# A feed-forward block on one Trainium2 core: a third set of raw weight buffers, Silu left in its PSUM bank, and a multiplication moved from GpSimd to VectorE

## The chip, the cores and the metric

The kernel runs on one core of a Trainium2 chip. The core has five engines that each follow their own list of instructions in order: TensorE (PE; its weight loads are listed apart as PEld), VectorE (DVE), ScalarE (ACT), GpSimd (POOL) and SyncE (SP), whose list here is almost only DMA issues. They wait for each other through semaphores. The time is device microseconds (us) of one execution; the number given for a kernel is the median of several runs.

## The reference

A trunk of two layers over 512 positions of width 1024, all in float32. Layer 0 has a sparse attention mixer, layer 1 a sliding-window mixer; behind each mixer stands the same feed-forward block, which is what the change touches:

```python
def causal_depthwise_conv(a, w, bias):
    ...  # over time, width 3, one filter per channel
    return y + bias.astype(a.dtype)

def conv_ffn(h, w_gu, conv_w, conv_b, w_down):
    a, u = jnp.split(h @ w_gu, 2, axis=-1)
    a = causal_depthwise_conv(a, conv_w, conv_b)
    return (jax.nn.silu(a) * u) @ w_down

for i in range(DEPTH):
    h = rms_norm(x, norm_mix[i])
    ...  # x = x + nsa_mixer(h, ...) in layer 0, x = x + swa_mixer(h, ...) in layer 1
    h = rms_norm(x, norm_ffn[i])
    x = x + conv_ffn(h, ffn_w_gu[i], ffn_conv_w[i], ffn_conv_b[i], ffn_w_down[i])
return rms_norm(x, norm_final)
```

`w_gu` is 1024 x 5632 (2816 columns for a, 2816 for u), `w_down` is 2816 x 1024.

## The kernel before

Activations lie transposed: features on the 128 partitions, the 512 positions along a row. Every float32 product is made from three products of rounded parts: an operand is split into a high part (rounded, written by ACT) and a low part (the difference to the original, written by DVE or POOL), and high x high, high x low and low x high are summed in PSUM.

The feed-forward block, function `ffn`, works on 22 tiles f of 128 channels of a and u. The first three (`PLAIN`) are done by `gate_up`, with whole 1024-row products (line L205). The other 19 are done by `gate_up_7`: the four half products of a tile (two halves of the positions by two halves of the input rows, for a and u) come from seven products over 256 positions (L619, 12 matmuls each, 84 for a unit) instead of eight, in the manner of Strassen and Winograd. One such tile is called a unit below. For a unit:

- `weights(f)` loads four raw quarter tiles a1, a2, u1, u2 of 128 x 512 (256 KB each, DMAs issued by SP, L591). POOL makes four sums and differences of them (L596): s1 = u1+u2, s2 = s1-a1, s3 = a1-u1, s4 = a2-s2. s2 and s3 share one buffer, named `wraw` in the rows.
- Each of the seven weights a1, s2, s3, a2, s1, s4, u2 is split: ACT writes the high part (L602: ha, wh, hs, hu), DVE the low part (L608: la, wl, ls, lu). For a1, a2 and u2 ACT first copies the raw weight to PSUM (L607), so that DVE reads one input from PSUM and one from SBUF; for s1, s2, s3, s4 (the rows ls and wl) DVE reads both inputs from SBUF. u2 is the last of the seven in program order.
- PE makes the seven products into the banks mm, s, t and o; ACT and DVE sum them into `apad` and into u's tile (L623, L629, L637; in the rows u's tile is called g, xh or xl).
- `activate` forms the convolution in a PSUM tile of the name t: one ACT instruction (L536) and two of DVE (L537, L538); then ACT applies Silu (L539) into an SBUF tile y, of which there is one buffer. At L649 (L555 in the plain units) POOL multiplies u by y.

All raw quarters have two buffers each (`BUFS`: a1, a2, u1, u2, and s1 and s4 too); `wraw` also has two. A DMA into a buffer waits until the last reader of the tile that lay there is done. Once the units are done, the low halves of the 22 gated tiles are put into the buffers that the weights have left, in the order of the list `GL`, and `down` multiplies by w_down.

The order of instructions on each engine isn't written out by hand: the framework's scheduler sets it when the kernel is built, from dependences, buffers and its own estimate of times. On the chip each engine keeps to its list, so an instruction that waits holds everything behind it on that engine.

Of the kernel before, what the change touches and what calls it, by code (L numbers as in the profile page):

```python
# [11 lines left out]
F32 = mybir.dt.float32  # L12
F32R = mybir.dt.float32r
AF = mybir.ActivationFunctionType
ALU = mybir.AluOpType
AX = mybir.AxisListType

P = 128
T = 512
# [38 lines left out]
PLAIN = (3, 3)  # L58
OPER = ((0, 1, 1, 1), (0, 1, 1, 1))
PLO = ((3, 6, 7), (3, 6))  # L60
BUFS = dict(a1=2, a2=2, u1=2, u2=2, s1=2, s4=2, ha1=2, la1=2, ha2=1, la2=1, hs1=1, ls1=1, hs4=1, ls4=1, hu2=1, lu2=1)
GL = [n for n in ("u1", "a1", "u2", "a2", "s1", "s4", "ha1", "la1", "ha2", "la2", "hs1", "ls1", "hs4", "ls4") for _ in range(BUFS[n])]
BANKS = dict(a1=("mm", B_MM), a2=("s", B_S), u2=("t", B_T))
CUES = (((), (0, 1), (2, 3, -1), (4, 5), (6, 7), (), ()), ((), (0, 1, 2), (3,), (4, 5, 6, -1), (7, 8), (), ()))
# [441 lines left out]
def ffn(tc, layer, e):  # L506
    nc, wp, ps, V = e["nc"], e["wp"], e["ps"], e["V"]
# [4 lines left out]
    with tc.tile_pool(name=f"ffn{layer}", bufs=1) as pool:  # L512
# [3 lines left out]
        def conv(i):  # L516
            return conv_t[:, i:i + 1]
# [4 lines left out]
        def gated(f):  # L522
            k = f - NF + len(x_tags)
            n = f"g{f}" if k < 0 else f"{x_tags[k][0]}{x_tags[k][1]}"
            g[f] = (pool if k < 0 else e["cp"]).tile([P, T], F32, name=n, tag=n)
            return g[f]
# [4 lines left out]
            nc.vector.memset(t[:, 0:2], 0.0)  # L531

        def activate(f, a):
            y = pool.tile([P, T], F32, name="y", tag="y", bufs=1)
            py = ps.tile([P, T], F32, name="t", tag="t", bufs=B_T)
            nc.scalar.activation(py, a[:, 2:], AF.Identity, scale=conv(f * 3 + 2), bias=conv(3 * NF + f))  # L536
            nc.vector.scalar_tensor_tensor(py, a[:, 1:T + 1], conv(f * 3 + 1), py, op0=ALU.mult, op1=ALU.add)  # L537
            nc.vector.scalar_tensor_tensor(py, a[:, 0:T], conv(f * 3), py, op0=ALU.mult, op1=ALU.add)  # L538
            nc.scalar.activation(y, py, AF.Silu)  # L539
            return y  # L540

        def plain(f, j, tag):
            w = load_w(e["w_gu"][layer, j, f], DM, nc.gpsimd if 2 * f + j in PLO[layer] else None)
            with tc.issue_after(e["stats"].behind.ins) if f == 1 and j == 0 else nullcontext():
                return run_value(e["proj_steps"](w=w, tag=tag))

        def gate_up(f):
            pa = plain(f, 0, "mm") if f else e["first"][0]
            a = apad[f % 2]
            nc.vector.tensor_tensor(a[:, 2:], pa, rstd, op=ALU.mult)  # L550
            y = activate(f, a)
            pu = plain(f, 1, "s") if f else e["first"][1]
            u = gated(f)
            nc.vector.tensor_tensor(u, pu, rstd, op=ALU.mult)
            nc.gpsimd.tensor_tensor(u, u, y, op=ALU.mult)  # L555

# [2 lines left out]
        def half(n, dt=F32R):  # L561
            return pool.tile([P, T], dt, name=n, tag=n, bufs=BUFS[n])

# [23 lines left out]
        def weights(f):  # L587
            a1, a2, u1, u2, s1, s4 = (half(n, F32) for n in ("a1", "a2", "u1", "u2", "s1", "s4"))
            for j, h, w in ((0, 0, a1), (1, 0, u1), (1, 1, u2), (0, 1, a2)):
                with tc.high_priority(offset=100):  # L590
                    nc.sync.dma_start(w, e["w_gu"][layer, j, f, :, h * T:(h + 1) * T])  # L591
            s23, l23, h23 = (wp.tile([P, 2, T], t, name=n, tag=n) for n, t in (("wraw", F32), ("wl", F32R), ("wh", F32R)))
            s2, s3 = (s23[:, h] for h in range(2))
            for out, x, y, op in ((s1, u1, u2, ALU.add), (s2, s1, a1, ALU.subtract), (s3, a1, u1, ALU.subtract),
                                  (s4, a2, s2, ALU.subtract)):
                nc.gpsimd.tensor_tensor(out, x, y, op=op)  # L596
            ws = {1: (h23[:, 0], l23[:, 0]), 3: (h23[:, 1], l23[:, 1])}
            for o, n, w in ((0, "a1", a1), (1, None, s2), (3, None, s3), (5, "a2", a2), (2, "s1", s1), (6, "s4", s4),
                            (4, "u2", u2)):
                if n:  # L600
                    ws[o] = half("h" + n), half("l" + n)
                nc.scalar.copy(ws[o][0], w)  # L602
                if n in BANKS:

                    tag, bufs = BANKS[n]
                    w = ps.tile([P, T], F32, name=tag, tag=tag, bufs=bufs)
                    nc.scalar.copy(w, {"a1": a1, "a2": a2, "u2": u2}[n])  # L607
                nc.vector.tensor_tensor(ws[o][1], w, f32(ws[o][0]), op=ALU.subtract)  # L608
            return ws

        def gate_up_7(f, cue):
            ws = weights(f)
            pa, pb, pc, pd = (ps.tile([P, T], F32, name=n, tag=n, bufs=b)[:, :H]
                              for n, b in (("mm", B_MM), ("s", B_S), ("t", B_T), ("o", B_O)))

            def product(pt, o, start=False):
                ops = [(0, x, i) for i in range(NK // 2) for x in range(2)] + [(1, 0, i) for i in range(NK // 2)]
                for n, (w, x, i) in enumerate(ops):
                    nc.tensor.matmul(pt, ws[o][w][:, i * P:(i + 1) * P], xs[:, o, i, x], start=start and n == 0,  # L619
                                     stop=n == len(ops) - 1, skip_group_check=True)  # L620

            def add(dst, pt, src):
                nc.vector.tensor_tensor(dst, pt, src, op=ALU.add)  # L623

            a, u = apad[f % 2], gated(f)
            al, ar = a[:, 2:2 + H], a[:, 2 + H:]
            ul, ur = (u[:, c] for c in HALVES)
            product(pa, 0, True)
            nc.scalar.copy(ar, pa)  # L629
            cue(0)  # L630
            product(pb, 1, True)
            add(ul, pb, ar)
            cue(1)
            product(pc, 3, True)
            cue(2)
            product(pa, 5)
            nc.scalar.copy(al, pa)  # L637
            cue(3)
            product(pb, 2)
            add(ar, pb, ar)  # L640
            add(ur, pc, ar)
            cue(4)
            product(pd, 6, True)
            add(ar, pd, ar)
            cue(5)
            product(pc, 4)
            add(ul, pc, ul)
            cue(6)
            nc.gpsimd.tensor_tensor(u, u, activate(f, a), op=ALU.mult)  # L649

        prs = ps.tile([P, T], F32, name="t", tag="t", bufs=B_T)
        nc.scalar.copy(prs, rstd)
        for f in range(PLAIN[layer]):
            gate_up(f)
            for i in range(NK // 2):
                if OPER[layer][i] == f:
                    operands(i)
        for f in range(PLAIN[layer], NF - 1):
            gate_up_7(f, lambda n: None)
# [20 lines left out]
        def cue(n):  # L680
            for f in CUES[layer][n]:
                if f < 0:
                    w_down.append(load_down(0, -1 - f))
                else:
                    split_g(f)

        gate_up_7(NF - 1, cue)

        stats = Stats(e["pool"], nc.gpsimd, 3) if layer == 0 else Stats(pool, nc.gpsimd, 3)
# [875 lines left out]
```

## Time and profile before

| what | value |
|---|---|
| median of 3 runs | 1295.8 us (1295.52 to 1297.48) |
| profiled execution | 1297.73 us |
| its span, first to last instruction | 1295.9 us |
| granted TensorE clock, mean | 0.982 |
| PE busy | 1228.0 us (95%) |
| DVE busy | 939.0 us (72%) |
| ACT busy | 760.1 us (59%) |
| POOL busy | 604.7 us (47%) |

The shares are means over very different stages. The two feed-forward blocks begin at about 372 and 910 us of the span; in each the plain units and the preparation of operands come first, then 19 units of seven products, then the down projection. Each row of the trace names an engine, a line of the kernel, and output and input tiles (out<-in).

### The profile page before, as it was taken

How to read it: one execution, taken by the hardware profiler on the slowest of the kernel's cores; microseconds unless marked ns; L12 is line 12 of the kernel's file. 1: busy time of each engine (PE TensorE's matmuls, PEld its weight loads, DVE VectorE, ACT ScalarE, POOL GpSimd, SP SyncE). 2: the span in 40 equal slices, each digit the busy share in tenths (PEclk: the TensorE clock that was granted, in tenths of full speed). 3: DMA queues.
4: the chain of work that ended last, by engine and by line, in shares of the span. 5: the costliest groups of instructions: out<-in, count | busy, mean ns of one | idle time of the engine just before them, and what ended most of it. 6: DMA issues, size and time to landing. Idle time of an engine off the chain costs nothing.

```text
span 1295.9 us, 20370 instructions
## 1 busy us (share of the span) xinstructions
PE 1228.0 (95%) x7246; PEld 1058.7 (82%) x7246; DVE 939.0 (72%) x1799; ACT 760.1 (59%) x1584; POOL 604.7 (47%) x451
## 2 busy tenths in 40 slices
PE   7999999989998999999999998999989999999997
PEld 5867986877876999999888886778779999998886
DVE  6376777978688897999633367897888999994223
ACT  4276667767558666767422225866677676683222
POOL 4494554523239676664100137322577766730002
PEclk9999999989998999999999998999989999999999
DMA  5856635041232332332233345322423332223333
GB/s 196 227 159 191 199 103 153 26 142 37 62 104 99 95 103 92 104 92 62 80 99 90 108 156 157 106 82 90 132 75 97 98 106 92 81 69 90 95 101 122
DMA packets 66485, 141.70 MB, mean 109 GB/s; under 512 B 8528, under 2 KB 16976, under 8 KB 66384
## 3 DMA queue, kind: packets, MB, share of 16 engines
q1 hardware_dynamic: 65008, 139.25, 35.5%
q8 instruction: 57, 0.93, 0.3%
q10 hardware_dynamic: 1376, 1.15, 0.3%
q14 instruction: 44, 0.36, 0.1%
HBM read 123.14 MB, written 17.24 MB: 108 GB/s over the span
## 4 chain that ended last, share of the span: by engine, by line
PE 53%; DVE 19%; DMA 7%; POOL 7%; ACT 7%; issue 5%; SPq 1%; POOLq 0%; DVEq 0%; ACTq 0%
PE mm L205 29%; PE t L619 4%; PE s L619 3%; DVE wl L608 3%; PE mm L619 3%; DMA u<-in_w_gu 2%; PE s L1165 2%; POOL s L596 2%; DVE ls L608 2%; PE o L619 2%; PE o L1007 2%; PE t L1189 2%; POOL wraw L596 1%; DMA d<-rh 1%; PE o L1307 1%
## 5 line engine op out<-in xcount | busy, mean ns | idle before, releaser
L182 ACT CAST wh<-wraw 128x1024 fp32r<-128x1024 f32 (+3 forms) x132 | 122.2, 926 | 224.5 <-PE mm L205 139.2
L183 DVE TENSOR_TENSOR wl<-wraw,wh 128x1024 fp32r<-128x1024 f32 (+3 forms) x80 | 98.0, 1225 | 118.7 <-PE mm L205 72.2
L183 POOL TENSOR_TENSOR wl<-wraw,wh 128x1024 fp32r<-128x1024 f32 (+3 forms) x52 | 98.7, 1902 | 136.5 <-PE mm L205 67.2
L205 PE MATMUL mm<-xs,wh 128*128 128x512 f32 (+1 forms) x374 | 141.5, 382 | 0.0
L238 POOL TENSOR_TENSOR rt<-rt 128x512 f32<-128x512 f32 x22 | 31.5, 1430 | 192.2 <-ACT rt L232 192.0
L608 DVE TENSOR_TENSOR wl<-wraw,wh 128x512 fp32r<-128x512 f32 x76 | 97.2, 1282 | 18.8 <-ACT wh L602 18.6
L205 PE MATMUL mm<-xh,wh 128*128 128x512 f32 x248 | 102.1, 413 | 6.9 <-ACT wh L182 5.1
L205 PE MATMUL mm<-xl,wh 128*128 128x512 f32 x248 | 99.9, 404 | 2.1 <-DVE xl L306 2.0
L619 PE MATMUL mm<-xs,ha 128*128 128x256 f32 x608 | 92.5, 289 | 9.4 <-ACT apad L629 4.8
L619 PEld LDWEIGHTS mm<-xs,ha 128*128 128x128 f32 x608 | 81.8, 195 | 12.3 <-ACT apad L629 6.2
L205 PE MATMUL mm<-xs,wl 128*128 128x512 f32 (+1 forms) x374 | 90.6, 382 | 0.0
L602 ACT CAST wh<-wraw 128x512 fp32r<-128x512 f32 x76 | 46.8, 620 | 69.4 <-POOL wraw L596 57.2
L1175 ACT ACTIVATE p<-p,sm 128x128 f32<-128x128 f32 (+3 forms) x128 | 71.7, 562 | 20.1 <-DVE sm L1172 19.5
L205 PEld LDWEIGHTS mm<-xs,wh 128*128 128x128 f32 x374 | 70.3, 188 | 14.7
L608 DVE TENSOR_TENSOR ls<-s,hs 128x512 fp32r<-128x512 f32 x76 | 80.2, 1060 | 0.0
L205 PEld LDWEIGHTS mm<-xs,wl 128*128 128x128 f32 x374 | 67.7, 188 | 15.1
L1172 DVE CUSTOM_DVE_ANT_0 p<-s,cst 128x128 f32<-128x128 f32 (+3 forms) x128 | 58.3, 480 | 18.1 <-PE t L1189 10.4
L205 PE MATMUL mm<-xh,wl 128*128 128x512 f32 x248 | 67.7, 403 | 0.0
L596 POOL TENSOR_TENSOR s<-u,u 128x512 f32<-128x512 f32 x38 | 53.2, 1401 | 27.1 <-DMA u<-in_w_gu 21.5
L649 POOL TENSOR_TENSOR xl<-xl,y 128x512 f32<-128x512 f32 x16 | 29.6, 1852 | 77.4 <-ACT y L539 69.9
L205 PEld LDWEIGHTS mm<-xh,wh 128*128 128x128 f32 x248 | 48.5, 196 | 18.8 <-ACT wh L182 5.3
L596 POOL TENSOR_TENSOR s<-a,wraw 128x512 f32<-128x512 f32 x38 | 62.8, 1653 | 0.2
(369 smaller groups left out, 3689.1 us busy)
## 6 DMA issues: line engine op xcount, KB each, us to landing
u<-in_w_gu SPq DMA_DIRECT2D x76, 256.0 KB, 2.9
a<-in_w_gu SPq DMA_DIRECT2D x76, 256.0 KB, 2.8
wraw<-in_w_dn SPq DMA_DIRECT2D x34, 512.0 KB, 3.5
wraw<-in_w_nsa SPq DMA_DIRECT2D x19, 512.0 KB, 4.9
q<-d SPq DMA_DIRECT2D x32, 256.0 KB, 5.1
wraw<-in_w_dn SPq DMA_DIRECT2D x17, 384.0 KB, 3.1
wraw<-in_w_gu SPq DMA_DIRECT2D x12, 512.0 KB, 3.5
d<-rh SPq DMA_DIRECT2D x21, 256.0 KB, 2.2
```

The source lines that it names most:

```text
L182: nc.scalar.copy(wh[:, c], raw[:, c])
L183: (eng or lo_eng[0]).tensor_tensor(wl[:, c], raw[:, c], f32(wh[:, c]), op=ALU.subtract)
L205: nc.tensor.matmul(pt, ws[k][w], rs[k][r], start=first and i == 0, stop=last and i == len(ops) - 1, **kw)
L238: self.eng.tensor_tensor(self.acc, self.acc, sq, op=ALU.add)
L596: nc.gpsimd.tensor_tensor(out, x, y, op=op)
L602: nc.scalar.copy(ws[o][0], w)
L608: nc.vector.tensor_tensor(ws[o][1], w, f32(ws[o][0]), op=ALU.subtract)
L619: nc.tensor.matmul(pt, ws[o][w][:, i * P:(i + 1) * P], xs[:, o, i, x], start=start and n == 0, stop=n == len(ops) - 1, skip_group_check=True)
L649: nc.gpsimd.tensor_tensor(u, u, activate(f, a), op=ALU.mult)
L1007: nc.tensor.matmul(acc[0][:, j * P:], v2[:, 2 * j + br], pp[:, 4 * j:4 * j + NT - j, :], start=br == 0 and j == 0 and pp is pts[0][0], sto ...
L1172: nc.vector.tensor_tensor_reduce(pt[:, c], pss[:, c], mask[:, T - (c.stop - c.start):], -1.0, 3e38, ALU.add, ALU.min, st[:, u:u + 1])
L1175: nc.scalar.activation(pt[:, c], pt[:, c], AF.Exp, scale=-1.0, bias=st[:, u:u + 1], accum_out=st[:, 2 + u:3 + u])
```

## The change

The four raw quarters get a third buffer each. Silu writes back into the PSUM tile that it reads, and the SBUF tile y is gone. The multiplication of u by it is issued by VectorE instead of GpSimd, in the plain units and in the units of seven products. A scratch area for dynamic DMAs is made smaller when the program is built, which leaves room in SBUF. `GL` is made from `BUFS`, so its first twelve places are now the raw quarters, and hs1, ls1, hs4 and ls4 are no longer used for low halves.

```diff
-BUFS = dict(a1=2, a2=2, u1=2, u2=2, s1=2, s4=2, ha1=2, la1=2, ha2=1, la2=1, hs1=1, ls1=1, hs4=1, ls4=1, hu2=1, lu2=1)
+BUFS = dict(a1=3, a2=3, u1=3, u2=3, s1=2, s4=2, ha1=2, la1=2, ha2=1, la2=1, hs1=1, ls1=1, hs4=1, ls4=1, hu2=1, lu2=1)
...
         def activate(f, a):
-            y = pool.tile([P, T], F32, name="y", tag="y", bufs=1)
             py = ps.tile([P, T], F32, name="t", tag="t", bufs=B_T)
...
-            nc.scalar.activation(y, py, AF.Silu)
-            return y
+            nc.scalar.activation(py, py, AF.Silu)
+            return py
...
             nc.vector.tensor_tensor(u, pu, rstd, op=ALU.mult)
-            nc.gpsimd.tensor_tensor(u, u, y, op=ALU.mult)
+            nc.vector.tensor_tensor(u, u, y, op=ALU.mult)
...
-            nc.gpsimd.tensor_tensor(u, u, activate(f, a), op=ALU.mult)
+            nc.vector.tensor_tensor(u, u, activate(f, a), op=ALU.mult)
...
-    nc = bacc.Bacc("TRN2", target_bir_lowering=False, num_devices=1)
+    nc = bacc.Bacc("TRN2", target_bir_lowering=False, num_devices=1, dynamic_dma_scratch_size=4096)
```

Lines behind L539 have a number one smaller in the changed kernel (L648 for L649, L607 for L608). The lists of the two mixers stay as they were; inside the feed-forward blocks the scheduler orders anew. POOL's list before, two units in the middle of layer 0 (the numbers behind the names tell the tiles of one unit from those of the next):

```order
L596 TENSOR_TENSOR s4_5452<-a2_5448,wraw_5457 128x512
L649 TENSOR_TENSOR xh3_5198<-xh3_5198,y_5290 128x512
L596 TENSOR_TENSOR s1_5601<-u1_5599,u2_5600 128x512
L596 TENSOR_TENSOR wraw_5607<-s1_5601,a1_5597 128x512
L596 TENSOR_TENSOR wraw_5757<-a1_5747,u1_5749 128x512
L596 TENSOR_TENSOR s4_5602<-a2_5598,wraw_5607 128x512
L649 TENSOR_TENSOR xh4_5348<-xh4_5348,y_5440 128x512
L596 TENSOR_TENSOR s1_5751<-u1_5749,u2_5750 128x512
```

And POOL's list now, over about the same units:

```order
L595 TENSOR_TENSOR s1_5589<-u1_5587,u2_5588 128x512
L595 TENSOR_TENSOR wraw_5595<-s1_5589,a1_5585 128x512
L595 TENSOR_TENSOR wraw_5744<-a1_5734,u1_5736 128x512
L595 TENSOR_TENSOR s4_5590<-a2_5586,wraw_5595 128x512
L595 TENSOR_TENSOR s1_5738<-u1_5736,u2_5737 128x512
L595 TENSOR_TENSOR wraw_5744<-s1_5738,a1_5734 128x512
L595 TENSOR_TENSOR s4_5739<-a2_5735,wraw_5744 128x512
L595 TENSOR_TENSOR wraw_5893<-a1_5883,u1_5885 128x512
L595 TENSOR_TENSOR s1_5887<-u1_5885,u2_5886 128x512
```

The multiplication no longer stands between one unit's four sums and the next one's. DVE's list before, from one unit's low parts to the next one's:

```order
L608 TENSOR_TENSOR wl_5758<-wraw_5757,wh_5759 128x512
L623 TENSOR_TENSOR xh6_5648<-s_5645,apad0_3990 128x256
L537 SCALAR_TENSOR_TENSOR t_5591<-apad1_3991,conv_t_3988,t_5591 128x512
L538 SCALAR_TENSOR_TENSOR t_5591<-apad1_3991,conv_t_3988,t_5591 128x512
L623 TENSOR_TENSOR xh5_5498<-t_5496,xh5_5498 128x256
L608 TENSOR_TENSOR lu2_5639<-t_5641,hu2_5638 128x512
L608 TENSOR_TENSOR la2_5775<-s_5777,ha2_5774 128x512
L608 TENSOR_TENSOR la1_5915<-mm_5917,ha1_5914 128x512
L623 TENSOR_TENSOR apad0_3990<-s_5645,apad0_3990 128x256
L608 TENSOR_TENSOR ls1_5781<-s1_5751,hs1_5780 128x512
L623 TENSOR_TENSOR xh6_5648<-t_5646,apad0_3990 128x256
L608 TENSOR_TENSOR wl_5908<-wraw_5907,wh_5909 128x512
```

And DVE's list now, first up to the last sum into a unit's u, then from its multiplication on to the low parts of a later unit:

```order
L607 TENSOR_TENSOR ls4_5623<-s4_5590,hs4_5622 128x512
L607 TENSOR_TENSOR la2_5613<-s_5615,ha2_5612 128x512
L607 TENSOR_TENSOR wl_5745<-wraw_5744,wh_5746 128x512 x2
L622 TENSOR_TENSOR apad1_3991<-s_5484,apad1_3991 128x256
L607 TENSOR_TENSOR ls1_5619<-s1_5589,hs1_5618 128x512
L607 TENSOR_TENSOR la1_5752<-mm_5754,ha1_5751 128x512
L622 TENSOR_TENSOR xh5_5487<-t_5485,apad1_3991 128x256
L622 TENSOR_TENSOR apad1_3991<-o_5486,apad1_3991 128x256
L622 TENSOR_TENSOR xh6_5636<-s_5633,apad0_3990 128x256
L536 SCALAR_TENSOR_TENSOR t_5579<-apad1_3991,conv_t_3988,t_5579 128x512
L537 SCALAR_TENSOR_TENSOR t_5579<-apad1_3991,conv_t_3988,t_5579 128x512
L622 TENSOR_TENSOR xh5_5487<-t_5485,xh5_5487 128x256
```

```order
L648 TENSOR_TENSOR xh5_5487<-xh5_5487,t_5579 128x512
L607 TENSOR_TENSOR lu2_5627<-t_5629,hu2_5626 128x512
L607 TENSOR_TENSOR la2_5762<-s_5764,ha2_5761 128x512
L622 TENSOR_TENSOR apad0_3990<-s_5633,apad0_3990 128x256
L607 TENSOR_TENSOR ls1_5768<-s1_5738,hs1_5767 128x512
L607 TENSOR_TENSOR la1_5901<-mm_5903,ha1_5900 128x512
L622 TENSOR_TENSOR xh6_5636<-t_5634,apad0_3990 128x256
L607 TENSOR_TENSOR wl_5894<-wraw_5893,wh_5895 128x512
L622 TENSOR_TENSOR apad0_3990<-o_5635,apad0_3990 128x256
L607 TENSOR_TENSOR wl_5894<-wraw_5893,wh_5895 128x512
L607 TENSOR_TENSOR ls4_5772<-s4_5739,hs4_5771 128x512
```

The multiplication (L648) now stands in DVE's list behind the last sum into u; the low parts around it have changed places among each other and with the sums.

## Rows read from the trace of the kernel before

**Rows 1.** Busy time by stretch: us, PE, PEld, DVE, ACT, POOL, clock, DMA share, GB/s.

```profile
372.00:420.00 48.00, 40.97 (x200) 33.69 (x200) 39.88 (x58) 35.92 (x65) 34.98 (x31) 0.92 0.34 111
420.00:470.00 50.00, 50.00 (x409) 49.92 (x409) 42.22 (x70) 34.60 (x67) 34.39 (x24) 0.97 0.33 100
470.00:619.00 149.00, 140.83 (x1137) 137.49 (x1137) 134.18 (x199) 102.15 (x195) 95.26 (x62) 1.00 0.28 87
619.00:741.00 122.00, 122.00 (x530) 98.19 (x529) 49.37 (x54) 37.88 (x49) 13.54 (x9) 1.00 0.31 92
...
1012.00:1161.00 149.00, 141.93 (x1144) 138.06 (x1145) 138.20 (x198) 103.28 (x196) 96.60 (x63) 1.00 0.29 88
```

**Rows 2.** Waits, 470 to 619 us: who for whom, us in total, times, longest.

```profile
ACT wh L602 <- POOL wraw L596: 22.0, 11, 3.9
...
PE t L619 <- DVE xh L623: 3.1, 3, 1.4
```

**Rows 3.** POOL by form, 470 to 619 us: busy, mean ns | idle before, releaser.

```profile
L596 POOL TENSOR_TENSOR s<-u,u 128x512 f32<-128x512 f32 x12 | 17.5, 1455 | 7.6 <-DMA u<-in_w_gu 7.6
...
L649 POOL TENSOR_TENSOR xl<-xl,y 128x512 f32<-128x512 f32 x7 | 13.5, 1929 | 26.4 <-ACT y L539 22.7 <-DVE xl L623 3.7
L649 POOL TENSOR_TENSOR xh<-xh,y 128x512 f32<-128x512 f32 x7 | 9.1, 1298 | 18.6 <-ACT y L539 18.6
```

**Rows 4.** Chain that ended last, 569 to 579 us: start, us, what.

```profile
570.79 3.03 DMA u<-in_w_gu
...
573.89 1.71 POOL s L596
...
575.68 1.64 POOL wraw L596
...
577.99 1.09 DVE wl L608
```

**Rows 5.** DVE by form, 470 to 619 us.

```profile
L608 DVE TENSOR_TENSOR wl<-wraw,wh 128x512 fp32r<-128x512 f32 x25 | 34.3, 1370 | 8.1 <-ACT wh L602 8.1
L608 DVE TENSOR_TENSOR ls<-s,hs 128x512 fp32r<-128x512 f32 x26 | 29.3, 1130 | 0.0
L538 DVE SCALAR_TENSOR_TENSOR t<-apad,conv_t,t 128x512 f32<-128x512 f32 x14 | 10.6, 755 | 0.5
...
L608 DVE TENSOR_TENSOR la<-mm,ha 128x512 fp32r<-128x512 f32 x12 | 8.2, 684 | 1.2 <-ACT mm L607 1.2
...
L671 DVE TENSOR_TENSOR u<-g,xs 128x512 fp32r<-128x512 f32 x4 | 2.6, 680 | 0.0
```

**Rows 6.** DVE by form, 1012 to 1161 us.

```profile
L608 DVE TENSOR_TENSOR wl<-wraw,wh 128x512 fp32r<-128x512 f32 x25 | 35.2, 1407 | 4.0 <-ACT wh L602 4.0
L608 DVE TENSOR_TENSOR ls<-s,hs 128x512 fp32r<-128x512 f32 x26 | 31.7, 1222 | 0.0
```

**Rows 7.** DVE by form, 420 to 470 us.

```profile
L608 DVE TENSOR_TENSOR wl<-wraw,wh 128x512 fp32r<-128x512 f32 x10 | 10.6, 1071 | 3.2 <-ACT wh L602 3.2
L608 DVE TENSOR_TENSOR ls<-s,hs 128x512 fp32r<-128x512 f32 x11 | 9.0, 825 | 0.0
```

**Rows 8.** POOL in order of time, 561 to 568 us: start, us, instruction.

```profile
562.46 1.62 POOL L596 TENSOR_TENSOR wraw<-s,a 128x512 f32<-128x512 f32 x1
```

**Rows 9.** DVE in order of time, 561 to 568 us.

```profile
561.19 0.69 DVE L608 TENSOR_TENSOR la<-mm,ha 128x512 fp32r<-128x512 f32 x1 [0.20 <-ACT mm L607]
561.80 1.13 DVE L608 TENSOR_TENSOR ls<-s,hs 128x512 fp32r<-128x512 f32 x1
562.86 1.77 DVE L608 TENSOR_TENSOR wl<-wraw,wh 128x512 fp32r<-128x512 f32 x1
```

**Rows 10.** Silu's instructions: ns shortest/median/longest.

```profile
L539 ACT ACTIVATE y<-t x44: 584/597/600, 393.6 to 1174.0; 128x512 f32<-128x512 f32 x44
```

**Rows 11.** Chain that ended last, 393 to 408 us.

```profile
394.57 0.65 DVE xs L585
...
406.49 0.60 DVE la L608
```

## The prediction

> **What bounds the kernel now.** I read the table of busy time by stretch first, to see where PE has idle time to give back. In the down projection it has none: 122.00 of 122 us [rows 1]. In the first units of seven products it has none either (50.00 of 50). It has some at the head of the block (48 - 40.97 = 7.0 us) and in the later units: 149 - 140.83 = 8.2 us in layer 0 and 149 - 141.93 = 7.1 us in layer 1 [rows 1]. These last two stretches, 15.3 us together, are where the change can gain; nothing else that it touches leaves PE idle, except the head.
>
> What does PE wait for there? The waits put PE behind DVE's sums (PE t <- DVE xh, 3.1 us) and show ACT standing 22.0 us before the high parts of s2 and s3, for POOL [rows 2]. DVE is the fullest engine beside PE: 134.18 of 149 us in layer 0 and 138.20 in layer 1 [rows 1]. Of its idle 14.8 and 10.8 us, 8.1 and 4.0 stand before wl, the low part of s2 or s3 [rows 5, 6]. So two things make DVE late: weights that POOL brings late, and DVE's own work.
>
> POOL is late for two reasons [rows 3]. It stands 26.4 + 18.6 = 45 us of 149 before the multiplication, nearly all of it for Silu, and the next unit's sums stand behind that instruction in its list. And it stands 7.6 us before s1, for the DMA of u2. The chain shows this second loop whole [rows 4]: the DMA into u2's buffer is issued only when the unit that last lay there has been read, takes 3.03 us, and then s1 (1.71), s2 (1.64) and wl (1.09) follow one after another.
>
> DVE's own work is swollen. Where both inputs come from SBUF, an instruction over 512 elements takes 680 ns when POOL does nothing (the split of the gated tiles), but 1370 (wl) and 1130 (ls) in the later units [rows 5], and 1407 and 1222 in layer 1 [rows 6]. With one input in PSUM it takes 684 whatever POOL does [rows 5]. One pair shows how: s2 runs on POOL from 562.46 to 564.08 [rows 8]; wl, whose turn on DVE comes at 562.93 when ls ends, ends at 564.63, some 0.55 us after POOL's instruction [rows 9]. The two don't run side by side.
>
> **The change, part by part.**
>
> *The multiplication on DVE.* The later stretch holds 14 of them (one for each L538 [rows 5]). The trace shows no DVE multiplication with one input in SBUF and one in PSUM. The nearest row is la<-mm, a subtraction with the same two places, 684 ns; the far one is wl at 1370, if it were caught by POOL [rows 5]. I take 684. Consecutive DVE instructions overlap by some 0.07 us (561.19 + 0.69 ends after 561.80 [rows 9]), so a place in the list costs 0.62 us: 14 x 0.62 = 8.7 us for each layer's later stretch. At the far end it would be 14 x 0.69 = 9.7 us more in each. In the early units DVE is busy 42.22 of 50 us while PE loses nothing [rows 1], so five multiplications more (3.1 us) are hidden behind PE there.
>
> [...]
>
> *Silu in its bank.* The instruction now writes PSUM instead of SBUF. Before it takes 597 ns [rows 10]; the conv's DVE step into the same bank takes 755 [rows 5]. Even at that price it is 0.16 us on ACT, which is busy 102 of 149 us [rows 1]; below, it may save a few ns. I take nothing. The bank is now held until DVE has multiplied, about 1.3 us longer, and is wanted again one unit later; nothing waits for it. The new wait of DVE for Silu has one sum of 0.35 us (step) in front where the list runs L536, L537, L622, L648, and low parts too in other units; 0 to 0.4 us a unit, and what queues behind is the next low parts. I count 0.1 a unit, 1.4 a stretch.
>
> *POOL without the multiplication, raw weights with a third buffer.* POOL's 45 us of standing for Silu and its 7.6 us for u2 go; u2's DMA now waits for the unit before the one that held it up. What is late next is the release of s1, s4 and wraw by DVE, which still have two buffers: POOL then runs two units ahead of DVE and waits for DVE, not DVE for it. So DVE's 8.1 and 4.0 us before wl go. I leave it the rest of its idle time, 14.8 - 8.1 = 6.7 and 10.8 - 4.0 = 6.8 us.
>
> *How DVE and POOL then meet.* This is the largest unknown. What POOL adds to DVE now is 25 x (1.370 - 0.68) + 26 x (1.130 - 0.68) = 29.0 us in layer 0 [rows 5] and 25 x 0.727 + 26 x 0.542 = 32.3 us in layer 1 [rows 6], about 2.2 and 2.5 us a unit over 13 units. Before, POOL's four sums begin right after its multiplication, just when DVE comes to the next ls and wl. In the new lists POOL waits for ls1 instead. In the first of the two pieces of DVE's new list, ls4, wl, wl and ls1 come while POOL waits, and after ls1 DVE has some 5 us of sums, conv and low parts from PSUM in front of it while POOL makes its four: they hardly meet, 0 us. In the second piece POOL makes s1 and s2 after ls1_5768 while DVE comes to wl, the sum, and wl: with 1.30 us for a POOL instruction [rows 3] and 0.55 us behind it, the two wl cost 0.3 and 0.8 us extra, up to 1.1 and 0.8 if u2 lands later, and ls4 0 to 1.3: 1.1 to 3.2 us. In a third kind of unit, where ls4 stands ahead of the pair, the same walk gives 2.3 to 3.1. The mean is 1.1 to 2.1; I take 1.6, so 13 x 1.6 = 21 us a stretch, 8 us less than now in layer 0 and 11 in layer 1. The bounds: the early units show what it is when POOL is ahead, 10 x 0.39 + 11 x 0.145 = 5.5 us in 50 [rows 7], 16.4 in 149, or 12.6 and 15.9 us less; at the other end it stays as it is.
>
> *The head of the block.* There the chain runs on DVE without a break from 394.57 to 407.09 us [rows 11], and two multiplications (f = 0 and 1) come into that piece: 2 x 0.62 = 1.2 us a layer, 2.5 in all. POOL's operands come a little sooner, and the third set's four DMAs now precede the last plain weight on SP's queue: I bound this between -1 and +5 us.
>
> *The sum.* Layer 0: 134.2 + 8.7 + 1.4 - 8 + 6.7 = 143.0 us for DVE against PE's 140.8: the stretch ends 149 - 143 = 6 us sooner. Layer 1: 138.2 + 8.7 + 1.4 - 11 + 6.8 = 144.1, 4.9 us sooner. Less 2.5 at the heads: 8.4 us. The profiled execution took 1297.73 us (1295.9 of span and 1.8 around it), so 1289.3; it lies 1.9 us above the median of the runs shown, so against that 1287.
>
> **The rivals.**
>
> 1. *PE alone bounds the later units*, as in the early ones. For it: PE lost nothing there at the lower contention [rows 1, 7]. Against it: DVE has 14 instructions more than it had then. Time: 15.3 us off with the head at no cost, 1295.8 - 15.3 = 1280.5.
> 2. *The gain is paid back on DVE.* The waits for POOL go, but contention falls by some 4 us a stretch only: 134.2 + 8.7 + 1.4 - 4 + 6.7 = 147.0 and 151.1, that is 2.0 sooner and 2.1 later, and the head 2.5 later: 1298, or 1295 with a free head.
> 3. *Slower: DVE becomes the bound.* POOL's four sums fall on DVE's ls and wl as now, and DVE carries the multiplication on top: 134.2 + 8.7 + 1.4 + 6.7 = 151.0 and 155.1, 2.0 and 6.1 us longer, with the head 10.6: 1306. It decides from where contention falls by less than about 5 us a stretch (some 0.4 us a unit). [...]
> 4. *The third set does nothing*, since s1, s4 and wraw keep two buffers and hold POOL as before. Then DVE's waits stay too, and the multiplication comes on top: about 1310. Against it: POOL's waits before are for Silu and for u2 [rows 3], none of note for those three.
>
> **How the numbers follow.** Forecast 0.50 (own range 1282 to 1293), rival 1 0.14, rival 2 0.15, rival 3 0.17, rival 4 0.04. The measurement tells 0.2% apart, about 2.6 us. The forecast and rival 1 are faster, with a little of rival 2: 0.67. Same is most of rival 2: 0.14. Slower is rivals 3 and 4 and a rest: 0.19. The range from 1279 to 1304 takes in rivals 1 and 2 and the nearer part of 3. The far price of the multiplication (19 us in all) is left outside it.
>
> **What would show it.** L648 at about 0.68 us on DVE, 44 times. POOL's idle time before s1 put down to DVE's ls, not to DMA or ACT. DVE's wait before wl near zero. The mean of wl and ls lower than now: near 1.1 us together, a mean of 1.4 or more would be rival 3. PE busy about 97 to 98% of the later units. The down projections and both mixers should keep their lengths. I am wrong if DVE is full in the later units and PE's idle time there has grown, or if the head takes over 3 us more.

## The result and the profile after

The changed kernel took 1283.95 us, the median of six runs (1279.12 to 1288.06); the kernel before took 1295.74 on the same chip (1290.75 to 1297.48). The ratio is 0.9912, with a 95% interval of 0.9885 to 0.9938: about 11.8 us, or 0.9%, faster. The forecast was 1287.

The profiled execution took 1279.85 us, 17.9 less than the one of before. To see which part of that is the change's, I cut both traces at the first DVE instruction of each norm (L277), which begins each mixer and each feed-forward block; the second block is taken to the end of the span. The two feed-forward blocks are 5.56 and 7.01 us shorter (370.78 to 365.22, 372.09 to 365.08): 12.6 us. The other 5.3 us lie in the mixers and in what stands ahead of the first cut, whose lists did not change, and are treated at the end.

Here is the busy time by stretch of the changed kernel, the same columns as [rows 1]. Its second block begins some 11 us earlier, so the last stretch is put 11 us earlier than there.

```profile
420.00:470.00 50.00, 48.46 (x379) 48.11 (x380) 45.72 (x73) 33.87 (x64) 28.54 (x21) 0.94 0.33 105
470.00:619.00 149.00, 147.75 (x1202) 145.46 (x1200) 137.33 (x224) 109.92 (x207) 64.12 (x47) 1.00 0.26 80
619.00:741.00 122.00, 121.80 (x523) 97.61 (x523) 46.77 (x50) 35.22 (x43) 11.09 (x7) 1.00 0.33 101
1001.00:1150.00 149.00, 147.43 (x1198) 144.57 (x1197) 137.62 (x227) 109.89 (x206) 63.35 (x46) 1.00 0.27 83
```

PE is busy 147.75 and 147.43 of 149 us in the later units (99%, where 97 to 98% was forecast); it was 140.83 and 141.93 [rows 1]. DVE carries more work than in layer 0 before (137.33 against 134.18) and about as much in layer 1 (137.62 against 138.20), though it has 13 and 14 multiplications more. POOL fell from 95 to 64 us.

POOL by form, 470 to 619 us (busy, mean ns | idle before, releaser), answers to [rows 3]:

```profile
L595 POOL TENSOR_TENSOR s<-u,u 128x512 f32<-128x512 f32 x12 | 15.6, 1296 | 47.9 <-DVE ls L607 45.2 <-DMA u<-in_w_gu 2.8
```

The standing for Silu is gone with the instruction, and the wait for the DMA of u2 fell from 7.6 us to 2.8, all of it in one place. POOL now stands 45.2 us for DVE to read the last s1: it is ahead of DVE. DVE by form in the same stretch answers to [rows 5]:

```profile
L607 DVE TENSOR_TENSOR wl<-wraw,wh 128x512 fp32r<-128x512 f32 x26 | 29.6, 1161 | 0.0
L607 DVE TENSOR_TENSOR ls<-s,hs 128x512 fp32r<-128x512 f32 x27 | 21.6, 805 | 0.7 <-ACT hs L601 0.7
...
L648 DVE TENSOR_TENSOR xh<-xh,t 128x512 f32<-128x512 f32 x7 | 4.7, 678 | 0.2
```

The 8.1 us before wl are 0.0. wl fell from 1370 to 1161 ns and ls from 1130 to 805. The multiplication costs 678 ns. Silu, by its instructions' duration (shortest/median/longest), costs no more in PSUM (582 ns) than its 597 ns in SBUF [rows 10]:

```profile
L538 ACT ACTIVATE t<-t x44: 576/582/593, 393.9 to 1153.6; 128x512 f32<-128x512 f32 x44
```

### The profile page after: what moved, and what is told of

It is laid out like the page before. It is cut to its first block, busy times and chain, and to the rows that moved or that the text cites. A ratio compares the mean times of both kernels' runs of the same rounds, so it can differ in the third digit from the quotient of the medians.

```text
span 1278.1 us, 20410 instructions
## 1 busy us (share of the span) xinstructions
PE 1219.4 (95%) x7246; PEld 1054.0 (82%) x7246; DVE 939.5 (74%) x1843; ACT 762.6 (60%) x1584; POOL 517.5 (40%) x407
## 4 chain that ended last, share of the span: by engine, by line
PE 66%; DVE 19%; issue 4%; DMA 4%; ACT 3%; POOL 3%; SPq 0%; POOLq 0%; DVEq 0%; ACTq 0%
PE mm L205 30%; PE mm L618 7%; PE s L618 7%; PE t L618 6%; PE o L618 3%; DVE wl L607 3%; PE s L1164 2%; PE o L1006 1%; PE t L1188 1%; DVE wl L183 1%; PE s L205 1%; DVE xs L584 1%; PE o L1306 1%; DVE xl L306 1%; DVE p L1183 1%
## 5 line engine op out<-in xcount | busy, mean ns | idle before, releaser
L618 PE MATMUL mm<-xs,ha 128*128 128x256 f32 x608 | 94.4, 289 | 7.6 <-DVE la L607 4.0
L618 PEld LDWEIGHTS mm<-xs,ha 128*128 128x128 f32 x608 | 82.8, 195 | 9.8 <-DVE xs L584 4.7
L607 DVE TENSOR_TENSOR wl<-wraw,wh 128x512 fp32r<-128x512 f32 x76 | 89.6, 1203 | 1.3 <-ACT wh L601 1.3
L1174 ACT ACTIVATE p<-p,sm 128x128 f32<-128x128 f32 (+3 forms) x128 | 71.7, 562 | 20.7 <-DVE sm L1171 20.2
L607 DVE TENSOR_TENSOR ls<-s,hs 128x512 fp32r<-128x512 f32 x76 | 63.0, 831 | 1.7 <-ACT hs L601 1.7
L205 PEld LDWEIGHTS mm<-xl,wh 128*128 128x128 f32 x248 | 47.2, 190 | 14.9 <-DVE xl L306 6.3
L595 POOL TENSOR_TENSOR wraw<-s,a 128x512 f32<-128x512 f32 x38 | 57.1, 1503 | 2.7
L535 ACT ACTIVATE t<-apad,conv_t 128x512 f32<-128x512 f32 x44 | 34.4, 783 | 37.0 <-DVE apad L622 32.5
```

The source lines that it names most:

```text
L205: nc.tensor.matmul(pt, ws[k][w], rs[k][r], start=first and i == 0, stop=last and i == len(ops) - 1, **kw)
L1174: nc.scalar.activation(pt[:, c], pt[:, c], AF.Exp, scale=-1.0, bias=st[:, u:u + 1], accum_out=st[:, 2 + u:3 + u])
```

## The experiments

One measure serves all of them. A unit has 84 matmuls, and the chain of the changed kernel shows twelve in 1.44 us (`PE s L618 x12`), 0.12 us each. From the first matmul of the third unit to the first of the nineteenth there are 16 x 84 = 1344, and in every execution where PE shows no idle time there they take 160.2 to 160.9 us. I call this stretch "16 units", what lies ahead of it from the norm on "head", and what lies behind it (the last unit and the down projection) "rest". All are read from the profiled execution, layer 0 / layer 1; the medians and ratios are of timed runs against the kernel before on the same chip.

| kernel | median us | ratio to before [95%] | head | 16 units | rest |
|---|---|---|---|---|---|
| before | 1295.7 | 1 | 53.7 / 53.9 | 173.1 / 172.7 | 144.1 / 145.6 |
| changed | 1284.0 | 0.9912 [0.9885, 0.9938] | 56.1 / 54.8 | 164.3 / 164.1 | 144.8 / 146.2 |
| changed, again | 1281.6 | 0.9918 [0.9888, 0.9949] | 54.8 / 55.9 | 164.8 / 164.7 | 144.8 / 146.3 |
| all third buffers, nothing else | 1276.6 | 0.9862 [0.9824, 0.9900] | 53.4 / 55.1 | 163.3 / 160.6 | 145.2 / 146.9 |
| the same, again | 1276.2 | 0.9875 [0.9852, 0.9899] | 53.8 / 53.7 | 163.2 / 160.6 | 145.2 / 146.8 |
| multiplication and Silu moved, two buffers | 1292.2 | 0.9990 [0.9966, 1.0013] | 55.1 / 57.2 | 171.2 / 171.3 | 143.9 / 145.6 |
| third buffer for u2 alone | 1271.0 | 0.9835 [0.9801, 0.9868] | 54.4 / 52.6 | 162.7 / 160.6 | 144.1 / 145.2 |
| the same, again | 1273.0 | 0.9838 [0.9813, 0.9863] | 54.3 / 53.9 | 162.6 / 160.5 | 144.2 / 145.2 |
| third buffers for a1, a2, u1 alone | 1294.8 | 1.0000 [0.9975, 1.0024] | 54.4 / 54.6 | 172.1 / 172.1 | 143.9 / 145.2 |
| changed, third buffer for u2 alone | 1282.3 | 0.9911 [0.9886, 0.9936] | 56.2 / 54.7 | 164.0 / 163.0 | 144.3 / 145.8 |
| changed, Silu into SBUF | 1287.1 | 0.9934 [0.9912, 0.9956] | 56.7 / 56.8 | 165.6 / 165.3 | 144.1 / 146.0 |
| changed, plain units' multiplication on POOL | 1279.9 | 0.9898 [0.9867, 0.9930] | 54.1 / 54.5 | 164.2 / 163.2 | 144.8 / 146.5 |
| changed, without POOL's sums (one run) | 1266.9 | – | 54.2 / 53.2 | 160.9 / 160.2 | 143.9 / 145.3 |

**The two halves of the change, each alone.** My theory gave both a share: the move frees POOL of its standing for Silu, the third set ends the loop of u2. The rivals give all of it to one half.

```diff
 # the third set alone: the kernel before, and
-BUFS = dict(a1=2, a2=2, u1=2, u2=2, ...
+BUFS = dict(a1=3, a2=3, u1=3, u2=3, ...
+    nc = bacc.Bacc(..., dynamic_dma_scratch_size=4096)
 # the move alone: the changed kernel, and
-BUFS = dict(a1=3, a2=3, u1=3, u2=3, ...
+BUFS = dict(a1=2, a2=2, u1=2, u2=2, ...
-    nc = bacc.Bacc(..., dynamic_dma_scratch_size=4096)
```

> The kernel before with the third set of raw buffers alone; the multiplication stays on GpSimd and Silu writes y in SBUF. Theory (the two parts work together: the third set ends the loop over u2's DMA, and taking the multiplication out of GpSimd's list lets GpSimd run ahead, so that its sums meet VectorE's ls and wl less often): GpSimd still stands some 40 us a stretch of 149 for Silu and still makes its four sums right after it, so ls and wl stay near 1.1 and 1.4 us; only the waits for u2 (7.6 and 6.3 us) and a part of VectorE's waits before wl go: 1289 to 1294 us. Rival (the third set alone is the gain, the move costs VectorE time that it gives back): the whole 12 us or more: 1280 to 1285 us.

> The changed kernel with two buffers of each raw quarter as before: Silu in its bank and the multiplication on VectorE alone. Theory (both parts needed): GpSimd no longer stands for Silu but now stands for u2's DMA before s1 (20 us or more a stretch), and VectorE carries the multiplication; contention falls a little: 1288 to 1295 us. Rival (the third set alone is the gain): VectorE's 8.7 us a stretch come on top of before: 1300 us or more. Second rival (the move alone is the gain): 1283 to 1286 us.

The third set alone is better than both together: 0.9862 and 0.9875 against 0.9912 and 0.9918. It also beat both of its expectations, 1289 to 1294 and 1280 to 1285 us. The intervals of single runs touch here; with u2's buffer alone, below, they do not. The move alone gives nothing (0.9990), as the busy time by stretch shows (470 to 619 and 1001 to 1150 us, columns as in [rows 1]) and POOL by form, 470 to 619 us:

```profile
470.00:619.00 149.00, 144.43 (x1153) 140.57 (x1152) 142.66 (x218) 107.97 (x202) 70.43 (x47) 1.00 0.28 88
...
1001.00:1150.00 149.00, 142.40 (x1167) 139.64 (x1165) 142.83 (x213) 104.38 (x198) 76.77 (x51) 1.00 0.30 94
```

```profile
L595 POOL TENSOR_TENSOR s<-u,u 128x512 f32<-128x512 f32 x12 | 15.8, 1316 | 54.3 <-DMA u<-in_w_gu 51.6 <-DVE lu L607 1.6 <-DVE xh L648 1.0
```

POOL, freed of Silu, stands 51.6 us for the DMA of u2 instead of 7.6 [rows 3]. The wait did not go: it changed its name. What holds the DMA is seen on SP's queue, in the waits of the same kernel and stretch (who for whom, us in total, times, longest):

```profile
SPq L590 <- ACT hu L601: 52.4, 11, 7.0
```

hu is the high part of u2, the last of the seven weights in program order. With two buffers the DMA for the unit after next is issued only then. In the kernel before the same row has 40.8 us. The chain that ended last [rows 4] shows the loop: ACT's hu, the DMA, POOL's s1 and s2, DVE's wl.

**Which third buffer.** If this is the loop, u2 needs the third buffer and the other three do not.

```diff
 # u2 alone (the kernel before, scratch area as in the change)
+BUFS = dict(a1=2, a2=2, u1=2, u2=3, ...
 # the other three alone
+BUFS = dict(a1=3, a2=3, u1=3, u2=2, ...
```

> The kernel before with a third buffer for u2 alone. Theory (what the third set buys is the end of one loop: u2 is read last in its unit, so its DMA is issued late, and s1, s2, the casts and wl stand behind it): as fast as with all four, 1275 to 1280 us; GpSimd's wait for u2's DMA (10 us in fifteen units before) falls under 4. Rival (GpSimd runs ahead only if all four quarters are there early): half the gain or less, 1285 to 1293 us, with GpSimd then standing for a1, a2 or u1.

> The kernel before with a third buffer for a1, a2 and u1, and two for u2. Theory (u2's loop): no gain to speak of, 1290 to 1297 us, with GpSimd still standing for u2's DMA. Rival (all four share in it): 1283 to 1289 us. Second rival (the gain comes from the order that the scheduler finds once there is more room, not from a particular buffer): anything, also 1277 us.

The other three alone are worth nothing (1.0000), and u2 alone is worth everything: 0.9835, about 22 us. The other three come with the smaller scratch area too, so that isn't the gain either. POOL by form with u2's third buffer, 470 to 619 us:

```profile
L596 POOL TENSOR_TENSOR s<-u,u 128x512 f32<-128x512 f32 x11 | 15.0, 1366 | 21.2 <-DVE ls L608 20.4 <-DMA u<-in_w_gu 0.9
...
L649 POOL TENSOR_TENSOR xl<-xl,y 128x512 f32<-128x512 f32 x7 | 11.0, 1569 | 25.8 <-ACT y L539 16.6 <-DVE xl L623 9.0
L649 POOL TENSOR_TENSOR xh<-xh,y 128x512 f32<-128x512 f32 x7 | 9.1, 1302 | 5.4 <-ACT y L539 5.4
```

and its busy time by stretch:

```profile
470.00:619.00 149.00, 148.17 (x1175) 144.41 (x1174) 135.31 (x209) 106.41 (x201) 79.40 (x57) 1.00 0.28 88
1001.00:1150.00 149.00, 149.00 (x1178) 145.45 (x1177) 133.12 (x207) 106.01 (x200) 76.97 (x57) 1.00 0.28 88
```

POOL still stands 31.2 us at the multiplication (25.8 + 5.4), 22.0 of them for Silu, and PE has 0.8 and 0.0 us of idle time. Once u2 has its third buffer, POOL's standing for Silu costs PE nothing: in the 16 units POOL isn't on the chain that ended last at all. SP's queue still stands 33.4 us for ACT's hu in this stretch, yet POOL's wait for the DMA is 0.9 us, so the queue's wait cost time only while there were two buffers.

One rival is left. The scheduler orders the lists anew when a buffer is added, and with u2's third buffer the lists of PE, DVE, ACT and POOL in the feed-forward blocks all differ from before. With the other three they hardly change: ACT's and POOL's are those of before, instruction for instruction. The second rival on record, that the gain comes from the order that the scheduler finds, is therefore not out. The runs show what u2's buffer and the order made for it are worth together; no run has the one without the other.

POOL's contention with DVE (what DVE's wl and ls take above the 0.68 us that they take with POOL silent, shown below) fell too, although POOL does all that it did before. DVE by form in this kernel, 470 to 619 us:

```profile
L608 DVE TENSOR_TENSOR wl<-wraw,wh 128x512 fp32r<-128x512 f32 x24 | 27.6, 1172 | 0.0
L608 DVE TENSOR_TENSOR ls<-s,hs 128x512 fp32r<-128x512 f32 x26 | 26.0, 1001 | 0.0
```

wl falls to 1172 ns, as far as with the move, in a kernel where POOL is ahead and waits for DVE's ls (20.4 us). Only ls gains from the move as well (805 against 1001).

**What the moved multiplication costs.** On one chip I ran the u2 buffer with the move and without, and all four buffers without.

```diff
 # the changed kernel, and
-BUFS = dict(a1=3, a2=3, u1=3, u2=3, ...
+BUFS = dict(a1=2, a2=2, u1=2, u2=3, ...
```

> The changed kernel with the third buffer for u2 only. Theory (the third buffer of u2 is the whole gain, the moved multiplication costs some 5 us on top of it): about 1278 us, within 4 us of the changed kernel and 4 to 8 us above the kernel before with u2's third buffer alone; PE's idle time in the later units 2 to 3 us, DVE's mean for ls about 0.86 us. Rival (the multiplication costs nothing; the three other third buffers are what cost the changed kernel its 5 us): equal to the kernel before with u2's third buffer alone, 1271.

> The kernel before with the third buffer for u2 alone, once more, on one chip with the next and the last kernel. If u2's buffer is the whole gain: 1271, and within 3 us of the kernel with all four third buffers. If the three others cost something: 4 to 6 us below it, as the first two runs on different chips had it.

> The kernel before with all four third buffers, multiplication on GpSimd, once more. If u2's buffer is the whole gain and the rest is free: within 3 us of the kernel with u2's buffer alone, about 1272 to 1276. If the three other buffers cost something: 1276 or more, 4 to 6 us above it.

1282.32 with the move against 1272.97 without: the move costs 9.3 us there, more than the 4 to 8 that I expected. (PE's idle time is 1.9 and 1.8 us in the 16 units and ls takes 805 ns in layer 0, both a little less than expected.) The profiled blocks are 3.4 and 3.9 us longer with it; the head takes 1.9 and 0.8 of that, the 16 units 1.4 and 2.5, the rest 0.1 and 0.6. The remaining 2 us of the medians have no place that I can show. The full third set costs 3.2 us over u2 alone (1276.21), at the edge of what these runs tell apart, with 1.0 and 1.6 us in the rest; the cause stays open.

**POOL's sums.** Is the cost of the move DVE's work itself, or DVE's meetings with POOL? This kernel leaves out POOL's four sums and uses raw tiles in their places, so that it computes other products.

```diff
-            s2, s3 = (s23[:, h] for h in range(2))
-            for out, x, y, op in ((s1, u1, u2, ALU.add), (s2, s1, a1, ALU.subtract), ...
-                nc.gpsimd.tensor_tensor(out, x, y, op=op)
+            s1, s2, s3, s4 = u2, a1, u1, a2
```

> The changed kernel without GpSimd's four sums for a unit: raw weights stand in their places, so the products are other ones. If GpSimd's sums are what stretches DVE's low parts: ls and wl take 0.68 us each, PE has no idle time in the later units, and units 2 to 18 of each layer take 161 us, some 3.5 us less than now: about 1275. If DVE itself is the bound whatever GpSimd does: PE's idle time stays at 2 to 3 us a layer, 164 us.

It took 1266.85 us, further down than I expected. DVE by form, 470 to 619 us, and busy time by stretch:

```profile
L604 DVE TENSOR_TENSOR wl<-u,wh 128x512 fp32r<-128x512 f32 x12 | 8.2, 684 | 0.0
...
L604 DVE TENSOR_TENSOR ls<-u,hs 128x512 fp32r<-128x512 f32 x12 | 8.2, 682 | 0.0
```

```profile
470.00:619.00 149.00, 149.00 (x1176) 145.57 (x1175) 123.10 (x220) 107.44 (x198) 0.00 (x0) 1.00 0.25 80
...
1001.00:1150.00 149.00, 149.00 (x1169) 145.05 (x1168) 122.03 (x217) 106.92 (x196) 0.00 (x0) 1.00 0.25 79
```

With POOL silent the same subtractions take 684 and 682 ns, and PE has no idle time in either stretch, with all multiplications on DVE. The blocks are 6.3 us shorter than in the changed kernel: 2.0 and 1.5 in the head, 3.5 and 3.9 in the units, 0.8 and 0.9 in the rest. So DVE has room for the multiplication by itself; it is short of it beside POOL's sums. Leaving the sums out also lets the weights come sooner, and this run doesn't part the two. In the changed kernel, though, DVE stands only 0.7 us before ls and none before wl, so the stretched low parts (15.9 us in layer 0) are the larger effect.

**Silu in PSUM or SBUF, and the head.** Two variants of the changed kernel: Silu into the SBUF tile y, still multiplied by DVE; and the six multiplications of the plain units back on POOL.

```diff
 # Silu into SBUF
+            y = pool.tile([P, T], F32, name="y", tag="y", bufs=1)
-            nc.scalar.activation(py, py, AF.Silu)
+            nc.scalar.activation(y, py, AF.Silu)
 # plain units (Silu into y there)
-            nc.vector.tensor_tensor(u, u, y, op=ALU.mult)
+            nc.gpsimd.tensor_tensor(u, u, y, op=ALU.mult)
```

> The changed kernel with Silu written to the SBUF tile y again, so that VectorE's multiplication has two SBUF inputs. Theory (two SBUF inputs wait for GpSimd's running instruction): the multiplication takes 1.0 to 1.4 us instead of 0.68 where GpSimd makes its sums beside it, 5 to 9 us a stretch more on VectorE, of which PE's bound hides some: 1286 to 1293 us. Rival (VectorE has enough slack now that it waits for PE): no difference, 1283 to 1285 us, with the multiplication at 0.68 to 1.4 us.

> The changed kernel with the three plain units' multiplication on GpSimd again (Silu into y there); the 19 later units keep it on VectorE. Theory (in the changed kernel the second unit of seven products starts 0.9 to 2.5 us later after the norm than before, since VectorE is the chain there and got the multiplications): that start comes back to 53 to 55 us after the norm in both layers, and the time falls by 2 to 4 us, to 1280 to 1282. Rival (the later start comes from the third set's DMAs in front of the last plain weight): it stays at 55 to 56 us, 1283 to 1285 us.

DVE by form of the first, 470 to 619 us:

```profile
L649 DVE TENSOR_TENSOR xh<-xh,y 128x512 f32<-128x512 f32 x7 | 5.9, 839 | 0.2
...
L649 DVE TENSOR_TENSOR xl<-xl,y 128x512 f32<-128x512 f32 x6 | 4.1, 686 | 0.2
```

The 839 ns are a mean over very different instructions. Of the 38 multiplications in the units, the two that run into one of POOL's instructions take 1.78 and 1.80 us, and the other 36 take 0.67 to 0.69, as with Silu in its bank (678). The blocks are 3 to 4 us longer together (734.4 against 730.3 and 731.2 in two executions of the changed kernel); the intervals of the ratios overlap, so the total alone does not show it. Moving the plain units' multiplications back gives heads of 54.1 and 54.5 us, where the changed kernel had 54.8 to 56.1 in two executions; its total is 1279.94 against 1281.58 on the same chip, within what the runs can tell.

**Both kernels once more.** The kernel before, profiled again, and the changed kernel, timed again, show how far one execution differs from the next.

> The kernel before, once more, for a second profile. In its first profile the second mixer took 171.6 us between its two norms, with PE standing 4.2 us at the first score product (L1378) for nothing that the trace names; in the changed kernel's profile it took 165.8 us without that stall, with the same instructions. If the stall is a matter of the execution, a second profile may lack it and the mixer then takes 166 to 168 us; if it belongs to the kernel's code as it lies in memory, it is there again at 171 to 172 us.

> The changed kernel once more beside the others, for a comparison on the same chip: 1281 to 1286 us. With the third set alone at 1276.6, theory (VectorE's multiplications cost the head and a little in the units what GpSimd would have done beside): 5 to 8 us slower than that. Rival (the difference was one between chips or calls): within 3 us of it.

The blocks of before came out at 372.6 and 372.1 us, with 173.9 and 172.2 for the 16 units, so the table's 8 to 12 us there are far outside the spread. The head is not: it varies by up to 1.4 us between executions of one kernel. The second mixer took 170.4 us in the repeat, between the two expectations, and decides for neither.

**A version that beats both** is the kernel before with u2's third buffer and the smaller scratch area alone: 0.9835 [0.9801, 0.9868] and 0.9838 [0.9813, 0.9863], against 0.9912 and 0.9918 for the changed kernel.

## Why the prediction was right, and where it was wrong

The time was right for a reason that was half wrong, and partly by luck: u2's buffer gained more than the sum gave to the whole change, and the move, which was to add to it, gave some of it back.

*The failed step: "POOL's 45 us of standing for Silu and its 7.6 us for u2 go", with the gain coming from both.* The second alone was enough. The 45 us [rows 3] are idle time of POOL, not time lost by PE. The kernel before had both loops on the chain that ended last. In the 16 units of each layer the chain passes four and five times through a DMA of u2, as in [rows 4], and twice from Silu through POOL's multiplication to s1. One of these, 526 to 531 us (start, us, what):

```profile
526.38 0.61 ACT y L539
...
527.05 1.29 POOL xh L649
528.34 1.71 POOL s L596
```

With u2's third buffer it passes through neither, although POOL still stands for Silu. With the move alone it still passes six and five times through a DMA of u2, and now also four and six times through DVE's multiplication. So the sum gave the third buffer no price of its own and counted on the move for a share of the gain. Alone the move is worth nothing that can be measured, and on top of the third buffer it costs 5 to 9 us.

*The room that PE had.* I took 15.3 us from busy time [rows 1] as all that could be gained. The same rows count the matmuls: 1137 at 0.12 us are 136 of 149 us, so 13 were lost in layer 0 where the busy column shows 8.2. By the 16 units, 173.1 and 172.7 against 160.6, it was 12.5 and 12.1, of which 8.2 and 7.6 stand in the trace as idle time. The rest hides in the matmuls' records: one lasts 0.28 us while the next starts 0.12 us after it, so a stop shows as idle time only beyond some 0.16 us, and these units have 34 and 40 places where two starts lie more than 0.14 us apart. The column beside it in [rows 1] says more: the weight loads (PEld) are busy 137.49 of the 149 us, 11.5 short. This is why the best version gains 22 us, and why rival 1's 1280.5 was no floor.

*The multiplication.* 0.684 us was forecast, 0.678 measured, in 38 units' instructions (0.669 to 0.690) and 6 plain ones; the far price does not occur with Silu in PSUM. No row of before showed that it could be left out of the range; that was an estimate from the nearest one, la<-mm at 684 ns [rows 5]. The six plain ones ran wholly beside POOL's instructions and took 0.67 us.

*Contention.* I predicted 29.0 falling to 21 us in layer 0. Measured: 26 x (1.161 - 0.68) + 27 x (0.805 - 0.68) = 15.9, better than forecast, just below the lower bound of 16.4. But u2's buffer without the move has 24 x (1.172 - 0.68) + 26 x (1.001 - 0.68) = 20.2. Most of the fall comes with the third buffer, where POOL is ahead, and the move adds about 4 us, half of the 8.7 that it costs. Single instructions in these runs: with POOL silent wl and ls took 684 and 682 ns; with one input in PSUM and POOL at work (64 of 149 us in the later stretch) none of the 38 multiplications took more than 690; with both in SBUF the two that ran into POOL's took 1.78 and 1.80 us.

*The sum.* It expected the later stretch 6 and 4.9 us sooner; the 16 units are 8.7 and 8.5 shorter. It treated DVE as full, 143 of 149 us with what it left of its idle time. DVE was busy 137.33 and stood 6.3 of the other 11.7 us for PE's products, so neither is full, and each stands for the other in turn; that leaves PE some 4 us above its 160.6.

*The head.* 1.2 us a layer were forecast for two multiplications in DVE's chain. They are there (395.32 and 403.98 in the chain after, 0.6 us each). The head is 2.5 and 0.9 longer than before in the first pair of profiles; over the six heads of the changed kernel (twice) and of the changed kernel with u2's buffer alone the mean is 55.4, over the twelve of before, of all third buffers and of u2 alone (each twice) 54.0: a difference of 1.4. The low parts are stretched there too. DVE and then POOL in order of time (start, us), 403 to 409 us of the changed kernel:

```profile
403.91 0.67 DVE L554 TENSOR_TENSOR g<-g,t 128x512 f32<-128x512 f32 x1
...
405.11 2.99 DVE L607 TENSOR_TENSOR wl<-wraw,wh 128x512 fp32r<-128x512 f32 x2
```

```profile
404.54 1.31 POOL L595 TENSOR_TENSOR wraw<-s,a 128x512 f32<-128x512 f32 x1
405.80 1.75 POOL L595 TENSOR_TENSOR wraw<-a,u 128x512 f32<-128x512 f32 x1
```

Two wl take 2.99 us where two undisturbed ones (684 ns each with POOL silent) would take 1.4, while POOL makes two sums. The first two wl of the kernel before took 1.85 us in layer 0 of its first profile and 2.4 in its other three blocks, so this place explains a part of the difference at most.

*The down projections* kept their lengths within 0.7 us, as said. *The third buffers of a1, a2 and u1* I priced at nothing, and they gave nothing.

*The rivals.* The third set doing nothing (4) and DVE as the bound (3) are out. Rival 2's "paid back on DVE" fits the move alone: its DVE is busy 142.7 and 142.8 of 149, the most of the kernels shown, its multiplication is on the chain, and the result is no change. (By its own terms rival 2 with a free head is 1296 us, not 1295.)

## What to carry to other kernels

Ask of each buffer when its last reader runs, not how many buffers a tile has: here the one that is read last in the loop was the one that wanted a third. An engine's largest wait need not be the one that decides: follow the chain, and ask what the engine would wait for next if that wait were gone, since the 45 us before the multiplication turned into 52 us before a DMA. Count instructions against their undisturbed length to learn what an engine has lost, because busy time can hide waiting (here PE's busy column shows 8.2 of the 12.5 us that it lost); and try the two halves of a change apart, since one can pay for the other (here u2's buffer gained some 22 us and the move gave back 5 to 9).

## What was not expected of the hardware

The mixers' lists are the same in all kernels, yet their lengths differ between executions: the sparse mixer took 348.5 to 358.4 us in the profiles here, the sliding-window one 165.8 to 171.6. One place is in the sliding-window mixer, before the first scores. PE in order of time (start, us, instruction, idle time before it in brackets), kernel before, 770 to 787 us:

```profile
786.34 0.44 PE L1378 MATMUL s<-kh,q 128*128 128x128 f32 x1 [4.18 <-issue]
```

The trace shows no wait behind these 4.18 us. At the same place the repeat of before stands 2.4 us, the changed kernel 1.5 in its first profile (put down to a DMA there) and 3.5 in its second. The granted clock of this mixer was 0.97 in the first profile of before and 1.00 in that of the changed kernel. The cause of the stop stays open. The mixers and what stands ahead of them make 5.3 of the 17.9 us between the first two profiles, which is why executions were compared by block and not by span.

The multiplication with two SBUF inputs, which the bound put at 1.37 us, took 0.84 at the most as a mean over a form: only two of the 38 in the units ran into one of POOL's, and these paid 1.78 and 1.80 us; the other 36 took 0.67 to 0.69.
